# Splitting ScalarE's top-k search into two chains that take turns

## The chip, the cores and the metric

The kernel runs on one core of a Trainium2 chip. The metric is the device time of one execution in microseconds (us), of which the median of several executions is given. A core has TensorE (PE in the profile, its weight loads PEld), VectorE (DVE), ScalarE (ACT), GpSimd (POOL) and SyncE (SP), which here issues the DMA transfers. Each engine works through its own queue in order; a queue whose first instruction waits holds everything behind it.

## The reference

Two transformer layers over 1024 tokens. Layer 0 mixes tokens by two attentions side by side. One of them (the part that matters here) lets each query see only the 256 keys with the highest indexer score:

```python
act = relu(einsum('bqhd,bsd->bqhs', qi, k_idx))
score = einsum('bqhs,bqh->bqs', act, wi)          # one row of up to 1024 scores per query
score = where(chunk_id(s) <= chunk_id(t), score, -inf)
_, sel = lax.top_k(score, 256)
...
o_b = diff_attention(...)                          # softmax(q0 k0) - lambda * softmax(q1 k1): two maps per head
y = concatenate([o_a, o_b]) @ w_out
```

Then, in both layers, follow an output projection, cross attention to a memory and an MLP.

## The kernel before

Queries are worked on in 8 blocks of 128 rows, one row per partition. The first two blocks have at most 256 admissible keys and need no search; the other six have score rows of 384, 512, 640, 768, 896 and 1024 numbers, which lie side by side in the tile `score`. `topk_steps` finds the 256th largest number of each row by a search over the 32 bits of its pattern, from the highest bit down. One bit takes a count over each row (how many scores reach the trial value) and then three tiny operations on VectorE which form the next trial value. `chain` is a generator of such a search over a list of blocks.

There are two chains. The d chain has the three short blocks; VectorE counts them itself (`dve_count`, L482). The a chain has the three long blocks; ScalarE counts them with a Sign activation and an accumulator (`act_count`, L486), and VectorE does the three updates (`tk_ok` L503, `tk_u` L510, `tk_try` L511). ScalarE's first count of a bit needs the `tk_try` of the bit before, and `tk_ok` needs all three counts. When the 32 bits are through, VectorE fixes the threshold (L526 to L534) and `select` makes the mask of each block (L550 to L555 on VectorE, L556 on GpSimd).

The search runs beside the projections of `even_rest`, which need no scores. TensorE does them in halves of 24 matmuls into four PSUM banks (`ps_S`); each half is split into a high part by ScalarE (`z_hi`, L135 or L129) and a low part by VectorE (`z_lo`, L136 or L130) and stored to DRAM by SyncE (L234, L235). The order of projections is qb (4), kb (4), with the small `ka` and `va` groups between, then eight tiles `vb` (L642), then qa (4). Their weights come in by DMA (L117), are rounded by ScalarE (`w_hi`, L120) and split by GpSimd (`w_lo`, L125). Between projections `pump` advances the chains by so many steps each.

Then come the attentions. `diff_units` come first: the scores of a unit are made for two maps one after the other (`scores`, L315, for `s0` and `s1`), reduced on VectorE (L332), exponentiated on ScalarE (L334), joined on GpSimd (L720, L725, L726) and turned by TensorE (L258). `load_qk` brings q and k of one map from DRAM in six transfers (L655 to L659).

What stands in an engine's queue is put in order, when the program is built, by a scheduler that estimates when each instruction could start. So a change in one place also changes the order around it. SBUF tiles of the attentions lie where tiles of the projections were, so a load may have to wait until TensorE is through with those.

Of the kernel before, what the change touches and what calls it, by code (L numbers as in the profile page):

```python
# [12 lines left out]
F32 = mybir.dt.float32  # L13
# [9 lines left out]
P = 128  # L23
# [7 lines left out]
TOPK = 256  # L31
# [37 lines left out]
class Net:  # L69
# [398 lines left out]
    def topk_steps(self, score, mask, offs, pool):  # L468
# [3 lines left out]
        nc = self.nc  # L472
        c = self.const
        nb = NT - BLK0
        ND = 3
        thr = c.tile([P, nb], F32, name="tk_thr")
        view = lambda j: score[:, offs[j + BLK0]:offs[j + BLK0] + P * (j + BLK0 + 1)]
        width = lambda j: P * (j + BLK0 + 1)

        def dve_count(j, t, op, acc):  # L480
            junk = pool.tile([P, 1024], BF16, name="tk_junk", bufs=1)
            nc.vector.tensor_scalar(junk[:, 0:width(j)], view(j), t, None, op0=op, op1=ALU.add, accum_out=acc)  # L482
# [5 lines left out]
        def chain(js, tag, count, limit):  # L488
            n = len(js)
            tr = [c.tile([P, n], I32, name="tk_try%d%s" % (i, tag)) for i in range(2)]  # L490
            ok = c.tile([P, n], I32, name="tk_ok" + tag)
            u = c.tile([P, n], I32, name="tk_u" + tag)
            cnt = c.tile([P, n], F32, name="tk_cnt" + tag)
            cur = tr[0]
            nc.vector.memset(cur, 0)
            for b in range(31, -1, -1):
                for k, j in enumerate(js):
                    count(j, cur[:, k:k + 1].bitcast(F32), cnt[:, k:k + 1])
                yield
                if limit is None:  # L500
                    nc.vector.tensor_scalar(ok, cnt, TOPK - 0.5, None, op0=ALU.is_ge)
                else:
                    nc.vector.tensor_tensor(ok, cnt, limit, ALU.is_le)  # L503
                if b == 31:
                    nc.vector.tensor_scalar(u, ok, 1.0, None, op0=ALU.subtract)
                    nxt = tr[1]
                    nc.vector.tensor_scalar(nxt, u, 1 << 30, None, op0=ALU.bitwise_xor)
                else:
                    nxt = tr[b % 2]
                    nc.vector.scalar_tensor_tensor(u, ok, b, cur, ALU.logical_shift_left, ALU.bitwise_xor)  # L510
                    nc.vector.tensor_scalar(nxt, u, 3 << (b - 1) if b > 0 else 1, None, op0=ALU.bitwise_xor)  # L511
                cur = nxt
                yield
            t = cur.bitcast(F32)
            if limit is None:
                nc.vector.tensor_copy(thr[:, js[0]:js[0] + n], t)
                yield
                for j in js:
                    select(j)
                    yield  # L520
                return

            gt = c.tile([P, n], F32, name="tk_gt" + tag)
            mn = c.tile([P, n], F32, name="tk_mn" + tag)
            for k, j in enumerate(js):
                dve_count(j, t[:, k:k + 1], ALU.is_gt, gt[:, k:k + 1])  # L526
                w = pool.tile([P, 1024], F32, name="tk_w", bufs=1)
                nc.vector.tensor_scalar(w[:, 0:width(j)], view(j), t[:, k:k + 1], 3e38, op0=ALU.is_le, op1=ALU.mult)
                nc.vector.tensor_tensor_reduce(w[:, 0:width(j)], w[:, 0:width(j)], view(j), 1.0, 3.3e38, ALU.add, ALU.min,
                                               accum_out=mn[:, k:k + 1])  # L530
                yield
            nc.vector.tensor_scalar(ok, gt, TOPK - 0.5, None, op0=ALU.is_ge)
            nc.vector.tensor_copy(thr[:, js[0]:js[0] + n], t)
            nc.vector.copy_predicated(thr[:, js[0]:js[0] + n], ok, mn)  # L534
            yield
            for j in js:
                select(j)
                yield
# [17 lines left out]
            nc.gpsimd.tensor_scalar(mask[:, offs[j + BLK0]:offs[j + BLK0] + n], gt[:, 0:n], -1.0, -NEG, op0=ALU.add,  # L556
                                    op1=ALU.mult)

        js_a = list(range(ND, nb))
        lim = c.tile([P, len(js_a)], F32, name="tk_lim")  # L560
        for k, j in enumerate(js_a):
            nc.vector.memset(lim[:, k:k + 1], float(width(j) - 2 * TOPK))
        return (chain(js_a, "a", act_count, lim),
                chain(list(range(ND)), "d", lambda j, t, acc: dve_count(j, t, ALU.is_ge, acc), None))

    def even_rest(self, act, zc, zp, z, topk):
        nc, A = self.nc, self.A

        def pump(*steps):

            for k in range(max(steps)):
                for chain, n in zip(topk, steps):
                    if k < n:
                        next(chain, None)

        def proj(name, k, sc, steps=(5, 6)):
            W = self.load_w(A["ev_fm"][k])
            z.setdefault(name, []).append(self.spill(lambda half: self.proj_half(W, act, half), sc, zp))
            pump(*steps)


        W = self.load_w(A["ev_fm"][5])
        uk = self.load_w(A["ev_uk_uv"], None, zc, 1)
        gkv = zc.tile([P, P], F32, name="gkv")
        nc.sync.dma_start(gkv, A["ev_a_kv_norm"][0:1, :].broadcast_to([P, P]))
        cT = zc.tile([P, S], F32, name="cT")
        for half in range(2):
            nc.scalar.activation(cT[:, half * 512:half * 512 + 512], self.proj_half(W, act, half), AF.Copy)
        ch = zc.tile([P, S], F32R, name="c_hi")
        cl = zc.tile([P, S], F32R, name="c_lo")  # L590
        for c in range(2):
            proj("qb", 6 + c, 0.125)
            pn = self.transpose4(cT[:, 512 * c:512 * c + 512], 4)
            q = self.small(4, name="cq")
            for j in range(4):
                junk = self.smallp.tile([P, 1024], BF16, name="junk", bufs=1)
                nc.scalar.activation(junk[:, 0:P], pn[:, j * P:(j + 1) * P], AF.Square, accum_out=q[:, j:j + 1])
            r = self.rstd(q, 4, 1.0 / P)
            cn = zc.tile([P, 512], F32, name="cn", bufs=1)
            for j in range(4):  # L600
                sl = slice(j * P, (j + 1) * P)
                nc.vector.scalar_tensor_tensor(cn[:, sl], pn[:, sl], r[:, j:j + 1], gkv, ALU.mult, ALU.mult)
            pt = self.transpose4(cn, 4)
            self.split(ch[:, 512 * c:512 * c + 512], cl[:, 512 * c:512 * c + 512], pt)
        z["ka"] = []
        z["va"] = self.dr([NT, P, 1024])

        def ka(p):
            def half_ps(half):
                ps = self.ps("S")  # L610
                sl = slice(half * 512, half * 512 + 512)
                self.mm3(ps, (uk[0][:, p * P:(p + 1) * P], uk[1][:, p * P:(p + 1) * P]), (ch[:, sl], cl[:, sl]), True, True)
                return ps

            z["ka"].append(self.spill(half_ps, 1.0, zp))

        def va(t):
            ps = self.ps("S")
            sl = slice(t * P, (t + 1) * P)
            self.mm3(ps, (ch[:, sl], cl[:, sl]), (uk[0][:, 512:1024], uk[1][:, 512:1024]), True, True)  # L620
            v = zc.tile([P, 8, P], F32R, name="va_st", bufs=2)
            self.split(v[:, :, 0:64], v[:, :, 64:128], ps.rearrange("p (h d) -> p h d", h=8))
            nc.sync.dma_start(z["va"][t], v.rearrange("p h d -> p (h d)").bitcast(F32))

        for k, (name, f, sc) in enumerate([("qb", 8, 0.125), ("qb", 9, 0.125)] + [("kb", 10 + j, 1.0) for j in range(4)]):
            proj(name, f, sc)
            if k < 4:
                ka(k)
                va(2 * k)
                va(2 * k + 1)  # L630
        Wv = [self.load_w(A["ev_vb"][j]) for j in range(4)]
        Wv = [[w.rearrange("p (k f) -> p k f", k=2) for w in pair] for pair in Wv]
        z["vb"] = self.dr([NT, P, 512])
        for t in range(NT):
            ps = self.ps("S")
            a = act[t // 4]
            sl = slice((t % 4) * P, (t % 4) * P + P)
            for kd in range(KD):
                w = Wv[kd // 2]
                self.mm3(ps, (a[0][:, kd, sl], a[1][:, kd, sl]), (w[0][:, kd % 2], w[1][:, kd % 2]), kd == 0, kd == KD - 1)  # L640
            v = zp.tile([P, 512], F32, name="vb", bufs=2)
            nc.scalar.activation(v, ps, AF.Copy)  # L642
            nc.sync.dma_start(z["vb"][t], v)
            pump(3, 4)
        for j in range(4):
            proj("qa", 14 + j, 0.125, (4, 2))
        pump(100, 100)

    def load_qk(self, zq, zk, j, pool):
        nc = self.nc  # L650
# [900 lines left out]
```

## Time and profile before

| | |
|---|---|
| time of the kernel before, median of 3 runs | 2593.91 us (2591.81 to 2595.8) |
| the profiled execution: its own time | 2590.76 us |
| its span, first to last instruction | 2589.0 us |
| busy: TensorE / VectorE / ScalarE / GpSimd | 2415.5 / 1687.6 / 1429.9 / 532.5 us |
| mean granted clock of TensorE | 0.97 of full speed |

Busy time is what an engine spent in its instructions. TensorE is busy for 93% of the span, so the question for any change is where TensorE stands idle, and what it waits for there. The times in the trace count from the start of the span; in each row the number in brackets is the idle time just ahead, with what ended it.

### The profile page before, as it was taken

How to read it: one execution, taken by the hardware profiler on the slowest of the kernel's cores; microseconds unless marked ns; L12 is line 12 of the kernel's file. 1: busy time of each engine (PE TensorE's matmuls, PEld its weight loads, DVE VectorE, ACT ScalarE, POOL GpSimd, SP SyncE). 2: the span in 40 equal slices, each digit the busy share in tenths (PEclk: the TensorE clock that was granted, in tenths of full speed). 3: DMA queues.
4: the chain of work that ended last, by engine and by line, in shares of the span. 5: the costliest groups of instructions: out<-in, count | busy, mean ns of one | idle time of the engine just before them, and what ended most of it. 6: DMA issues, size and time to landing. Idle time of an engine off the chain costs nothing. (4 is left out here: it accounts for less than half of the span.)

```text
span 2589.0 us, 34350 instructions
## 1 busy us (share of the span) xinstructions
PE 2415.5 (93%) x11493; PEld 1972.1 (76%) x11493; DVE 1687.6 (65%) x3184; ACT 1429.9 (55%) x2808; POOL 532.5 (21%) x898
## 2 busy tenths in 40 slices
PE   7999988899997799997999999989979999899998
PEld 6877867688876687875888878878757777688886
DVE  5599676698448755553655768874596555446556
ACT  5577747787356555552434458873565555434433
POOL 5322125545233000000000245541320000000003
PEclk9999989999998899998999999999989999999999
DMA  5225365663423344465776531123233443667665
GB/s 179 82 87 217 129 193 131 149 161 99 159 82 130 103 154 140 146 243 191 248 252 211 195 126 38 38 88 128 82 119 126 148 157 135 226 241 257 226 228 178
DMA packets 165662, 402.78 MB, mean 156 GB/s; under 512 B 20282, under 2 KB 38638, under 8 KB 165486
## 3 DMA queue, kind: packets, MB, share of 16 engines
q1 hardware_dynamic: 165486, 400.59, 46.9%
q8 instruction: 91, 1.49, 0.2%
q14 instruction: 85, 0.70, 0.1%
HBM read 283.47 MB, written 117.05 MB: 155 GB/s over the span
## 5 line engine op out<-in xcount | busy, mean ns | idle before, releaser
L200 POOL TENSOR_SCALAR rstd<-ssq 128x1 f32<-128x1 f32 x48 | 40.5, 844 | 1329.2 <-ACT junk L154 1328.3
L129 ACT ACTIVATE l_hi<-l_raw 128x1024 fp32r<-128x1024 f32 x112 | 118.5, 1060 | 344.2 <-PE ps_T L1259 147.4
L130 DVE TENSOR_TENSOR l_lo<-l_raw,l_hi 128x1024 fp32r<-128x1024 f32 x112 | 136.8, 1223 | 126.0 <-ACT l_hi L129 126.0
L1259 PE MATMUL ps_S<-w_hi,l_hi 128*128 128x512 f32 x480 | 191.4, 399 | 27.2 <-ACT l_hi L129 27.2
L125 POOL TENSOR_TENSOR w_lo<-w_raw,w_hi 128x512 fp32r<-128x512 f32 x118 | 159.5, 1374 | 237.5 <-ACT w_hi L120 221.6
L140 PE MATMUL ps_S<-act_hi,w_hi 128*128 128x512 f32 x512 | 201.6, 395 | 2.5 <-DVE z_lo L130 1.2
L141 PE MATMUL ps_S<-act_lo,w_hi 128*128 128x512 f32 x512 | 200.5, 392 | 1.5 <-DVE act_lo L130 1.5
L142 PE MATMUL ps_S<-act_hi,w_lo 128*128 128x512 f32 x512 | 199.4, 390 | 0.1
L1259 PE MATMUL ps_S<-w_hi,l_lo 128*128 128x512 f32 x480 | 189.0, 396 | 0.0
L1259 PE MATMUL ps_S<-w_lo,l_hi 128*128 128x512 f32 x480 | 188.7, 393 | 0.0
L129 ACT ACTIVATE s_hi<-w_raw 128x512 fp32r<-128x512 f32 x160 | 100.6, 631 | 100.3 <-PE ps_S L1100 83.6
L130 DVE TENSOR_TENSOR s_lo<-w_raw,s_hi 128x512 fp32r<-128x512 f32 x160 | 109.8, 688 | 58.6 <-ACT s_hi L129 45.6
L1259 PEld LDWEIGHTS ps_S<-w_hi,l_hi 128*128 128x128 f32 x480 | 91.6, 191 | 46.9 <-ACT l_hi L129 28.0
L140 PE MATMUL ps_S<-w_hi,act_hi 128*128 128x512 f32 x320 | 124.7, 398 | 2.4 <-DVE yn L198 1.5
L141 PE MATMUL ps_S<-w_lo,act_hi 128*128 128x512 f32 x320 | 126.2, 395 | 0.1
L142 PE MATMUL ps_S<-w_hi,act_lo 128*128 128x512 f32 x320 | 125.6, 393 | 0.0
L140 PEld LDWEIGHTS ps_S<-act_hi,w_hi 128*128 128x128 f32 x512 | 96.2, 188 | 24.4 <-DVE onm L1421 2.3
L141 PEld LDWEIGHTS ps_S<-act_lo,w_hi 128*128 128x128 f32 x512 | 96.3, 188 | 20.6 <-DVE act_lo L130 2.2
L142 PEld LDWEIGHTS ps_S<-act_hi,w_lo 128*128 128x128 f32 x512 | 96.2, 188 | 19.8 <-POOL w_lo L125 0.5
L334 ACT ACTIVATE s<-s,nm 128x128 f32<-128x128 f32 (+7 forms) x128 | 99.1, 778 | 19.3 <-DVE nm L332 18.9
L1259 PEld LDWEIGHTS ps_S<-w_hi,l_lo 128*128 128x128 f32 x480 | 91.2, 190 | 21.5
L1259 PEld LDWEIGHTS ps_S<-w_lo,l_hi 128*128 128x128 f32 x480 | 91.3, 190 | 20.4
(367 smaller groups left out, 7194.1 us busy)
## 6 DMA issues: line engine op xcount, KB each, us to landing
l_raw<-dr SPq DMA_DIRECT2D x112, 512.0 KB, 4.5
dr<-ua SPq DMA_DIRECT2D x192, 256.0 KB, 2.4
w_raw<-w SPq DMA_DIRECT2D x64, 512.0 KB, 3.6
w_lo<-w SPq DMA_DIRECT2D x128, 256.0 KB, 4.1
w_hi<-w SPq DMA_DIRECT2D x128, 256.0 KB, 4.6
x_dram<-xt SPq DMA_DIRECT2D x40, 512.0 KB, 2.9
xt<-x_dram SPq DMA_DIRECT2D x40, 512.0 KB, 3.7
w_raw<-ev_fm SPq DMA_DIRECT2D x18, 512.0 KB, 4.0
```

Source lines behind the costliest of these rows:

```text
L125: nc.gpsimd.tensor_tensor(lo[:, cs], raw[:, cs], hi[:, cs].bitcast(F32), ALU.subtract)
L129: self.nc.scalar.activation(hi, src, AF.Copy)
L130: self.nc.vector.tensor_tensor(lo, src, hi.bitcast(F32), ALU.subtract)
L140: nc.tensor.matmul(ps, lhsT=a[0], rhs=b[0], start=first, stop=False)
L141: nc.tensor.matmul(ps, lhsT=a[0], rhs=b[1], start=False, stop=False)
L142: nc.tensor.matmul(ps, lhsT=a[1], rhs=b[0], start=False, stop=last)
L200: nc.gpsimd.tensor_scalar(r, q[:, 0:1], q[:, 1:2] if n == 2 else 0.0, EPS, op0=ALU.add, op1=ALU.add)
L334: nc.scalar.activation(s[:, 0:n], s[:, 0:n], AF.Exp, bias=nm, scale=-1.0, accum_out=sm)
L1259: nc.tensor.matmul(banks[z][t], lhsT=x[i], rhs=w[j][:, e], start=start and b == 0 and e == 0 and n == 0, stop=b == NB - 1 and e == 1 and n ...
```

## The change

The a chain is cut in two. The new a chain has only the longest block (1024 numbers), the new b chain has the blocks of 768 and 896. `pump` advances a, b and d one step each in turn. The counts stay as they were; the three update operations are now done once for a and once for b in every bit.

```diff
-        js_a = list(range(ND, nb))
-        lim = c.tile([P, len(js_a)], F32, name="tk_lim")
-        for k, j in enumerate(js_a):
-            nc.vector.memset(lim[:, k:k + 1], float(width(j) - 2 * TOPK))
-        return (chain(js_a, "a", act_count, lim),
+        def signs(js, tag):
+            lim = c.tile([P, len(js)], F32, name="tk_lim" + tag)
+            for k, j in enumerate(js):
+                nc.vector.memset(lim[:, k:k + 1], float(width(j) - 2 * TOPK))
+            return chain(js, tag, act_count, lim)
+
+        return (signs([nb - 1], "a"), signs(list(range(ND, nb - 1)), "b"),
                 chain(list(range(ND)), "d", lambda j, t, acc: dve_count(j, t, ALU.is_ge, acc), None))
...
-        def proj(name, k, sc, steps=(5, 6)):
+        def proj(name, k, sc, steps=(5, 5, 6)):
...
-            pump(3, 4)
+            pump(3, 3, 4)
         for j in range(4):
-            proj("qa", 14 + j, 0.125, (4, 2))
-        pump(100, 100)
+            proj("qa", 14 + j, 0.125, (4, 4, 2))
+        pump(100, 100, 100)
```

The order of the queues shows three places. From line 566 on, the lines of the changed kernel stand two higher (L642 is L644 there).

ScalarE's queue in the middle of the search, before: one bit of the a chain is three counts in a row, and the next bit's counts (with the other trial tile) follow at once.

```order
L486 ACTIVATE tk_junk_a,tk_cnta<-score,tk_try0a 128x768
L486 ACTIVATE tk_junk_a,tk_cnta<-score,tk_try0a 128x896
L486 ACTIVATE tk_junk_a,tk_cnta<-score,tk_try0a 128x1024
L642 ACTIVATE vb<-ps_S 128x512
L486 ACTIVATE tk_junk_a,tk_cnta<-score,tk_try1a 128x768
```

The same place of ScalarE's queue now:

```order
L486 ACTIVATE tk_junk_a,tk_cnta<-score,tk_try1a 128x1024
L486 ACTIVATE tk_junk_a,tk_cntb<-score,tk_try1b 128x768
L486 ACTIVATE tk_junk_a,tk_cntb<-score,tk_try1b 128x896
L486 ACTIVATE tk_junk_a,tk_cnta<-score,tk_try0a 128x1024
L486 ACTIVATE tk_junk_a,tk_cntb<-score,tk_try0b 128x768
L486 ACTIVATE tk_junk_a,tk_cntb<-score,tk_try0b 128x896
L644 ACTIVATE vb<-ps_S 128x512
```

Between two counts of a there now stand the two of b, and the other way round. The end of the search has moved too: before, 11 of the 32 bits of a were still to come when the d chain was through, now it is 5 of a and 6 of b; the last count now stands ahead of three of the eight `vb` and of all four `w_hi` of the qa projections.

ScalarE's queue at the end of the search now:

```order
L486 ACTIVATE tk_junk_a,tk_cnta<-score,tk_try1a 128x1024
L486 ACTIVATE tk_junk_a,tk_cntb<-score,tk_try1b 128x768
L644 ACTIVATE vb<-ps_S 128x512
L486 ACTIVATE tk_junk_a,tk_cntb<-score,tk_try1b 128x896
L644 ACTIVATE vb<-ps_S 128x512 x2
L120 ACTIVATE w_hi<-w_raw 128x1024 x2
```

Before, the last six bits stood between and behind these `w_hi`, and the last count stood among the `z_hi` of qa. On VectorE the last operation of `select` stood behind the last `z_lo`, among the first reductions of the scores; now it stands ahead of the last six `z_lo`.

SyncE's queue at the loads of the second map of the first head, before (dr_1879 and dr_1880 are its q, dr_2499 and dr_2500 its k, dr_3599 the second qa projection, dr_3696 the third):

```order
L658 DMA att_kh<-dr_2499 64x1024
L655 DMA att_q<-dr_1879 64x1024
L234 DMA dr_3599<-z_hi 128x1024
L656 DMA att_q<-dr_1880 64x1024
L659 DMA att_kh<-dr_2499 64x1024
L235 DMA dr_3600<-z_lo 128x1024
L658 DMA att_kl<-dr_2500 64x1024
L659 DMA att_kl<-dr_2500 64x1024
L234 DMA dr_3696<-z_hi 128x1024
```

The same loads now (dr_1880 and dr_1881 are q, dr_2536 k, dr_3871 and dr_3872 the fourth and last qa projection):

```order
L660 DMA att_kh<-dr_2536 64x1024
L657 DMA att_q<-dr_1880 64x1024
L234 DMA dr_3871<-z_hi 128x1024
L235 DMA dr_3872<-z_lo 128x1024
L658 DMA att_q<-dr_1881 64x1024
L661 DMA att_kh<-dr_2536 64x1024
```

The second halves of q and k of that map have moved behind the store of the last qa projection's `z_lo`. TensorE's second pair of score matmuls waits for both of them.

## Rows read from the trace of the kernel before

**Rows 1.** Busy time of each engine in two stretches (start:end, length, then us).

```profile
core 0: us, PE busy (x) PEld busy (x) DVE busy (x) ACT busy (x) POOL busy (x), PEclk, DMA share, GB/s
160.00:346.00 186.00, 180.34 (x796) 147.19 (x795) 141.75 (x460) 145.15 (x272) 38.77 (x41) 1.00 0.45 158
160.00:289.00 129.00, 123.39 (x546) 100.36 (x545) 118.77 (x396) 101.05 (x192) 26.33 (x29) 1.00 0.48 178
```

**Rows 2.** Timeline of TensorE, end of projections (start, length, instruction, [idle before]).

```profile
364.94 0.39 PE L142 MATMUL ps_S<-act_hi,w_lo 128*128 128x512 f32 x1
365.17 0.28 PE L315 MATMUL ps_S<-att_kh,att_q 128*128 128x256 f32 x1
...
366.99 0.39 PE L315 MATMUL ps_S<-att_kh,att_q 128*128 128x256 f32 x1 [1.18 <-DVE tk_need L551]
...
374.57 0.58 PE L315 MATMUL ps_S<-att_kh,att_q 128*128 128x256 f32 x1 [7.08 <-DVE tk_need L551]
...
379.45 0.48 PE L258 MATMUL ps_T<-ident,s 128*128 128x128 f32 x1
```

**Rows 3.** Timeline of VectorE at the same place.

```profile
373.83 0.69 DVE L136 SCALAR_TENSOR_TENSOR z_lo<-ps_S,z_hi 128x512 fp32r<-128x512 f32 x1
...
374.49 0.28 DVE L332 CUSTOM_DVE_ANT_0 s<-ps_S,H 128x128 f32<-128x128 f32 x1
...
375.25 1.28 DVE L554 SCALAR_TENSOR_TENSOR tk_eq<-tk_w,tk_need,tk_eq 128x1024 bf16<-128x1024 f32 x1
```

**Rows 4.** Waits from 155 to 375 us (total us, times, longest).

```profile
DVE tk_oka L503 <- ACT tk_junk_a L486: 32.0, 18, 5.2
ACT tk_junk_a L486 <- DVE tk_try1a L511: 17.2, 14, 3.9
ACT tk_junk_a L486 <- DVE tk_try0a L511: 14.0, 10, 3.1
```

**Rows 5.** Timeline of ScalarE: a weight, a vb tile, first counts of two bits.

```profile
319.95 1.04 ACT L120 ACTIVATE w_hi<-w_raw 128x1024 fp32r<-128x1024 f32 x1
...
324.01 0.58 ACT L642 ACTIVATE vb<-ps_S 128x512 f32<-128x512 f32 x1
...
338.08 0.94 ACT L486 ACTIVATE tk_junk_a<-score,tk_try0a 128x768 bf16<-128x768 f32 x1 [0.21 <-DVE tk_try0a L511]
...
342.24 0.94 ACT L486 ACTIVATE tk_junk_a<-score,tk_try1a 128x768 bf16<-128x768 f32 x1 [0.69 <-DVE tk_try1a L511]
```

**Rows 6.** Timeline of VectorE: tiny operations of the chains among counts.

```profile
266.07 0.17 DVE L501 TENSOR_SCALAR tk_okd<-tk_cntd 128x3 int32<-128x3 f32 x1
...
266.68 0.61 DVE L482 TENSOR_SCALAR_CACHE_REDUCE tk_junk<-score,tk_try0d 128x384 bf16<-128x384 f32 x1
...
267.33 0.75 DVE L482 TENSOR_SCALAR_CACHE_REDUCE tk_junk<-score,tk_try0d 128x512 bf16<-128x512 f32 x1
...
268.00 0.16 DVE L503 TENSOR_TENSOR tk_oka<-tk_cnta,tk_lim 128x3 int32<-128x3 f32 x1
268.12 0.88 DVE L482 TENSOR_SCALAR_CACHE_REDUCE tk_junk<-score,tk_try0d 128x640 bf16<-128x640 f32 x1
...
270.99 1.21 DVE L510 SCALAR_TENSOR_TENSOR tk_ud<-tk_okd,tk_try0d 128x3 int32<-128x3 int32 x1
```

**Rows 7.** Timeline of GpSimd: weights of qa, then the first units.

```profile
321.08 5.05 POOL L125 TENSOR_TENSOR w_lo<-w_raw,w_hi 128x512 fp32r<-128x512 f32 x4 [18.57 <-ACT w_hi L120]
...
379.48 1.04 POOL L556 TENSOR_SCALAR mask<-tk_gt 128x1024 bf16<-128x1024 bf16 x1
...
382.38 0.72 POOL L726 TENSOR_TENSOR s<-s 128x256 f32<-128x256 f32 x1
```

**Rows 8.** SyncE's queue: timeline of two issues.

```profile
354.75 0.59 SPq L659 DMA_DIRECT2D att_kl<-dr  x1
...
374.54 0.33 SPq L235 DMA_DIRECT2D dr<-z_lo  x1
```

**Rows 9.** The tile att_q from 325 to 400 us: issue to landing.

```profile
DMA to landing us min/median/max: 4.7/5.1/7.7
```

## The prediction

> **What bounds the kernel now.** I read the page first: TensorE is busy for 93% of the span, so only its idle places can pay. The stretches around the search come next [rows 1]. From 160 to 346 us, while the search runs, TensorE is busy for 180.34 of 186 us: the search costs it almost nothing there. The 5.6 us that it lacks lie all before 289 us, in the `ka` and `va` groups. So a faster search is worth nothing by itself; what counts is what its end holds up. TensorE's timeline shows that [rows 2]: the last projection's matmul starts at 364.94, two pairs of scores follow, one more at 366.99, and then TensorE stands for 7.08 us until 374.57. VectorE's timeline gives the cause [rows 3]: the last `z_lo`, which frees a PSUM bank, starts at 373.83, and the first reduction of scores at 374.49. Up to there VectorE was busy with fixing thresholds and `select` for the three long blocks, which could only start when the a chain was through (about 346.5). The reductions wait in the same queue.
>
> The a chain is late because it runs at neither engine's pace. The list of waits [rows 4] has both sides: VectorE waited 32.0 us for counts, ScalarE 17.2 + 14.0 = 31.2 us for trial values, in 24 waits (1.3 us each).
>
> **The change, part by part.** *ScalarE's waits.* One bit of counts takes 342.24 − 338.08 − 0.69 = 3.47 us without the wait [rows 5], some 1.06, 1.17 and 1.24 us for the three widths. While VectorE updates a, ScalarE now counts b's two blocks (2.2 us), more than the mean wait; while it updates b, it counts a's one (1.24 us), about as much. So most of the 31.2 us goes. It is bounded by 31.2 (all of it) and 0; the long waits (up to 3.9) are only partly covered, and I leave 11 us, a third.
>
> *The end of the chain.* ScalarE was busy for 145.15 us from 160 to 346 [rows 1]. Of that, four `w_hi` (1.04 each), three `vb` and three `z_hi` (about 0.58 each) [rows 5], together 7.7, now stand behind the last count. Idle were 186 − 145.15 = 40.85; 31.2 of it by the chain, 9.65 by other things. So the last count ends at 160 + 137.5 + 9.65 + 11 = 318, bounded by 307 and 338 with none and all of the waits kept.
>
> *VectorE's 96 more tiny operations* (three a bit, 32 bits). Three of them in a row, each waiting for the last, take 266.68 − 266.07 = 0.61, so 0.20 each; one put between two counts costs nothing (a 512 count of 0.75 to the next count: 0.79 with `tk_oka` between; a 384 count of 0.61 to the next: 0.65 without) [rows 6]. That bounds the 96 by 0 and 19.5 us. Most stand between or beside others; I take 0.08 each, 7.7 us. Then the d chain ends at 289 + 8 = 297, and the 5.5 bits left, 5.5 × 3.47 and two `vb`, end at 317. The two ways agree; I take 318, between 307 and 338.
>
> *A row that speaks against it:* `tk_ud` at 270.99 took 1.21 instead of 0.16 us [rows 6], as long as one of GpSimd's four subtractions at 321.08 (5.05 / 4 = 1.26) [rows 7]. GpSimd was busy for 26.33 us of the d chain's 129 [rows 1], the most that such holding can take there. If the added operations were held for half of that, the chain would end 13 us later, at 331. The Trainium skill ("SBUF — State Buffer", section "Who interferes with whom") says that VectorE and GpSimd share a port pair as an exclusive lock, and that the second to start is blocked until the first is done; the 1.21 us agree with it. It makes a rival, below.
>
> *What the new place of the last count holds up.* Behind it stand two `vb`, then the first `w_hi` of qa, then GpSimd's subtraction of its first half: 318 + 2 × 0.58 + 1.04 + 1.26 = 321.5. TensorE needs them when qa begins: 8 halves of 24 matmuls at 180.34 / 796 = 0.2266 us [rows 1] are 43.5, so at 365.2 − 43.5 = 321.7, the low part half a us later. So there is no stall up to 318.8 for the last count; each us beyond costs one.
>
> *The end of the search.* From the last count to the end of `select` VectorE took some 32 us before (346.5 to 378.6, evictions included), so it now ends by about 350. The last `z_lo` follows its `z_hi` at once. TensorE's last matmul ends at 365.3, `z_hi` 0.6 later, so `z_lo` runs from 366.0 to 366.7 instead of 373.83 to 374.52: 7.8 us earlier.
>
> *What is late next.* The first unit needs the second map, and two of that map's loads now stand in SyncE's queue behind the store of that last `z_lo`. Before, the last load of that map was issued at 354.75 and the store, at 374.54, right when `z_lo` ended, held up nothing of it [rows 8]. Now: store at 366.7, `att_q` at 367.1, `att_kh` at 367.6, and 5.1 us to landing (4.7 to 7.7) [rows 9], so the second pair of scores starts at about 372.6 (371.8 to 374.8). Everything behind it on TensorE waits too. The removed wait of 7 us has a successor of almost the same length.
>
> *What is left.* Before, two more pairs had been made by then, so TensorE came from the fourth pair at 374.57 to the first turn of a unit at 379.45 [rows 2]. From 372.6 it has two pairs of some 0.5 us more and one at the end (0.45) less to do, so it comes there at about 378.0: 1.4 us earlier. The second unit gains more: `select`'s 1.28 us [rows 3] no longer stands among the reductions, and the mask of 1.04 us at 379.48 no longer stands ahead of GpSimd's joins [rows 7]. Its join, ended at 383.1 before, should end at about 378.5: 4.6 us. GpSimd paces the next units, and I take 3.5 us, between 1.4 and 4.6, as what lasts.
>
> *The sum:* 2590.76 − 3.5 + 0 (stall) = 2587.3 for the profiled execution, whose time is 3.15 below the median of the runs; against that median, 2593.91 − 3.5 = **2590.4 us**, 0.13% less. A difference under 0.2% (5.2 us) is about what a measurement here cannot tell from none.
>
> **The rivals.**
> - *The full gain.* Nothing takes the place of the wait: the loads come sooner than I think, or SyncE's queue is not held. Then the first reductions move with `z_lo`, and 374.49 − 365.6 = 8.9 us is gained: 2585.0. For it: VectorE's wait really goes. Against: the order of SyncE's queue. If the 5.6 us of the `ka` and `va` groups went too, 2579; but VectorE, whose `z_lo` they wait for, has more to do there, not less. Chance 0.25.
> - *The chain ends late (slower).* The tiny operations are held behind counts and behind GpSimd's subtractions, so ScalarE's waits stay. From 318.8 each us of delay stalls TensorE at the first qa weights. From 322.3 the gain is eaten, from 327.5 the kernel is slower by over 0.2%; at 331 (13 us of holding) it is 2593.9 − 3.5 + 12.2 = 2602.6. For it: the held `tk_ud` and the in-order queue. Against: VectorE was busy for 118.77 of 129 us [rows 1] with room for half of what is added, and the b chain's counts give each update 2.2 us. Chance 0.15. The lock that the Trainium skill states ("SBUF — State Buffer", "Who interferes with whom") would be what holds them.
> - *No gain at all.* The loads take the 7.7 us that one of them took, the second pair starts at 374.8, and the ramp is as before: 2593.9. The search is faster for nothing. Chance 0.15.
> - *My forecast:* 0.45.
>
> **How the numbers follow.** The likeliest case gives 2590.4, its own range 2588 to 2594. Eight in ten take in the full gain (2585, and a little below for the spread of the medians) and the first part of the late chain: 2583 to 2598. Faster by over 0.2%: the full gain and a bit of the forecast's edge, 0.28. Slower: the late chain, 0.15, less what of it ends before 327.5 and more for changes of order further on, 0.15. The rest, 0.57, is no change.
>
> **What the profile after would show.** Right: ScalarE's waits for trial values fall from 31 to about 11 us; the last count ends near 318; VectorE is through with `select` by 350; the last `z_lo` starts near 366; TensorE still stands for about 7 us after the first pair of scores, now for a load of `att_q` or `att_kh`. Wrong: a stall of TensorE at the first qa weights (late chain), or pairs of scores that follow the first without a gap (full gain), or more idle time in the `ka` and `va` groups than 5.6 us.

## The result, and the profile after

The changed kernel takes 2608.64 us (median of 4 runs, 2606.68 to 2609.68), the kernel before 2593.35 (4 runs, 2591.81 to 2595.8). The ratio is 1.0057, with a 95% interval of 1.004 to 1.0075: slower by 0.57%, some 15 us. The prediction was 2590.4, no change, in a range from 2583 to 2598. It was wrong.

The profiled execution took 2609.68 us, 18.9 more than the one of before (the medians are 15.3 apart, so some 3.6 of it belong to these two executions). Cut at the same places of the program in both traces (the first and last starts of a group of matmuls), the difference falls like this:

| stretch of TensorE | before | after | difference |
|---|---|---|---|
| start to the last indexer score | 158.8 | 160.1 | +1.3 |
| search beside projections, to the first attention score | 206.4 | 212.4 | +6.0 |
| attentions, to the last score | 257.5 | 257.6 | +0.1 |
| even output projection, to the first cross-attention score | 119.4 | 124.7 | +5.3 |
| the rest | 1846.9 | 1853.1 | +6.2 |

The last row holds several us that vary between executions: with the same order of instructions it was 1846.9 before, and 1851.9 (e7) and 1849.1 (e9) in two experiments below. The search and the output projection are the two that stand out, and the attentions, where something was to be gained.

First the search. In the waits of the kernel after from 155 to 375 us (total, times, longest) the chains do what the change says:

```profile
DVE tk_okb L503 <- ACT tk_junk_a L486: 6.3, 10, 2.0
...
ACT tk_junk_a L486 <- DVE tk_oka L503: 4.4, 6, 1.1
ACT tk_junk_a L486 <- DVE tk_ua L510: 3.7, 2, 2.5
...
DVE tk_oka L503 <- ACT tk_junk_a L486: 2.9, 6, 0.7
```

VectorE waits 9.2 us for counts instead of 32.0, ScalarE 10.8 us for the chain instead of 31.2 [rows 4] (the 8.1 of these lines and four more waits of 0.4 to 1.0). The busy times after, in the second stretch of [rows 1] and in two short ones (the column of 0.97 is the granted clock of TensorE; an x counts every instruction that overlaps the stretch):

```profile
160.00:289.00 129.00, 120.42 (x516) 96.96 (x515) 121.58 (x477) 114.39 (x218) 26.18 (x30) 0.97 0.45 166
210.90:214.30 3.40, 3.40 (x10) 2.63 (x9) 3.40 (x12) 3.21 (x8) 0.00 (x0) 0.51 0.62 213
262.10:265.50 3.40, 3.40 (x9) 2.63 (x10) 3.40 (x13) 1.00 (x2) 0.00 (x0) 0.51 0.85 201
```

Up to 289 us ScalarE is busy for 114.39 us, 13 more than before: the counts that used to come later come now. In the same 129 us TensorE made 516 matmuls instead of 546. ScalarE's timeline shows how the two hang together:

```profile
207.39 0.58 ACT L135 ACTIVATE z_hi<-ps_S 128x512 fp32r<-128x512 f32 x1
207.87 1.03 ACT L486 ACTIVATE tk_junk_a<-score,tk_try0b 128x896 bf16<-128x896 f32 x1
...
208.90 0.58 ACT L129 ACTIVATE z_hi<-ps_S 128x512 fp32r<-128x512 f32 x1
209.37 0.59 ACT L129 ACTIVATE c_hi<-ps_T 128x512 fp32r<-128x512 f32 x1
...
315.00 1.03 ACT L486 ACTIVATE tk_junk_a<-score,tk_try1b 128x896 bf16<-128x896 f32 x1
...
372.68 0.60 ACT L135 ACTIVATE z_hi<-ps_S 128x512 fp32r<-128x512 f32 x1 [4.84 <-PE ps_S L142]
...
663.81 1.06 ACT L120 ACTIVATE w_hi<-w_raw 128x1024 fp32r<-128x1024 f32 x1 [8.72 <-DMA w_raw<-ev_out]
```

A count of the b chain, whose trial value is there already, stands at 207.87 between two evictions. The `c_hi` at 209.37, which TensorE needs, ends one count later than it could. TensorE's timeline after, at this and later places:

```profile
210.02 0.50 PE L140 MATMUL ps_S<-c_hi,w_hi 128*128 128x512 f32 x1 [2.82 <-ACT c_hi L129]
...
228.23 0.50 PE L140 MATMUL ps_S<-w_hi,c_hi 128*128 128x512 f32 x1 [1.29 <-DVE z_lo L136]
...
261.96 0.66 PE L140 MATMUL ps_S<-act_hi,w_hi 128*128 128x512 f32 x1 [1.34 <-DVE z_lo L130]
...
265.71 0.40 PE L140 MATMUL ps_S<-act_hi,w_hi 128*128 128x512 f32 x1
...
372.48 0.28 PE L315 MATMUL ps_S<-att_kh,att_q 128*128 128x256 f32 x1
...
382.86 0.55 PE L315 MATMUL ps_S<-att_kh,att_q 128*128 128x256 f32 x1 [9.98 <-DMA att_kh<-dr]
...
664.91 0.80 PE L140 MATMUL ps_S<-w_hi,act_hi 128*128 128x512 f32 x1 [3.46 <-ACT w_hi L120]
...
1762.47 0.80 PE L140 MATMUL ps_S<-w_hi,act_hi 128*128 128x512 f32 x1 [5.35 <-DVE yn L198]
```

Six waits in the `ka` and `va` groups (2.82, 1.29, 0.88, 1.06, 0.93 and 1.34 us) make 8.3; before, five made 5.5 (1.25, 1.05, 1.05, 1.95 and 0.17). Behind the first and the last of the six the granted clock is 0.51 for 3.4 us, the lower of its two levels (1.2 of 2.4 GHz). The matmuls start 0.43 us apart there: nine steps from one start to the next take 3.75 us from 261.96 to 265.71, and nine take 3.65 from 210.82 to 214.47. At 0.2266 us a step the 18 would take 4.1 us, so 3.3 more are lost. 2.8 + 3.3 make up the 6.0. Before, the clock stayed at 1.00 in both places.

The counts are not the whole of it. Ahead of the last two of these waits VectorE's own queue is late:

```profile
257.69 2.53 POOL L125 TENSOR_TENSOR w_lo<-w_raw,w_hi 128x512 fp32r<-128x512 f32 x2 [12.86 <-ACT w_hi L120]
```

```profile
257.94 1.06 DVE L510 SCALAR_TENSOR_TENSOR tk_ua<-tk_oka,tk_try1a 128x1 int32<-128x1 int32 x1
258.92 0.68 DVE L130 TENSOR_TENSOR z_lo<-ps_S,z_hi 128x512 fp32r<-128x512 f32 x1
```

The `z_hi` of this half is through at 258.10. But `tk_ua`, which takes 1.06 us where most take 0.16, ends only when the first of GpSimd's two subtractions does (257.69 + 1.26), and `z_lo` starts at 258.92; TensorE's wait of 0.93 us at 259.65 is for it. Ahead of the last wait it is a held `tk_okd` (0.72 us) and a count of 0.61 us that stand before the `z_lo`. From 200 to 270 us five such operations took 3.5 us more than usual after the change, two took 1.7 before.

VectorE's timeline after has the other end of the search:

```profile
208.90 1.18 DVE L510 SCALAR_TENSOR_TENSOR tk_ud<-tk_okd,tk_try1d 128x3 int32<-128x3 int32 x1
...
349.02 0.62 DVE L555 TENSOR_TENSOR tk_gt<-tk_gt,tk_eq 128x896 bf16<-128x896 bf16 x1
...
373.31 0.69 DVE L136 SCALAR_TENSOR_TENSOR z_lo<-ps_S,z_hi 128x512 fp32r<-128x512 f32 x1
...
1761.72 1.29 DVE L198 TENSOR_TENSOR yn<-ps_S,g 128x512 f32<-128x512 f32 x2 [4.98 <-DMA g<-norm_g]
```

`select` is through at 349.6, and the last `z_lo` follows its `z_hi` (372.68) at once. Nothing of the search holds up the first scores any more, [rows 3] are gone. But at the handover from the projections to the scores the wait of 7.08 us in [rows 2] has become one of 9.98 us, up to 382.86, for `att_kh`. SyncE's queue after, at this place and ahead of the output projection (an entry with x6 is six issues of one line in a row):

```profile
372.45 0.45 SPq L660 DMA_DIRECT2D att_kh<-dr  x1
372.99 0.55 SPq L657 DMA_DIRECT2D att_q<-dr  x1
373.63 0.54 SPq L234 DMA_DIRECT2D dr<-z_hi  x1
374.21 0.42 SPq L235 DMA_DIRECT2D dr<-z_lo  x1
374.69 0.45 SPq L658 DMA_DIRECT2D att_q<-dr  x1
375.19 1.32 SPq L661 DMA_DIRECT2D att_kh<-dr  x1
...
629.87 0.33 SPq L159 DMA_DIRECT2D g<-norm_g  x1
630.79 18.89 SPq L117 DMA_DIRECT2D w_raw<-ev_out  x6
...
651.37 8.13 SPq L934 DMA_DIRECT2D xk<-dr  x8
659.61 0.52 SPq L117 DMA_DIRECT2D w_raw<-ev_out  x1
```

Even the two loads of the second map that stand *ahead* of the stores are issued only at 372.45, when the last projection's matmuls end; the two stores then take 1.1 us of the queue (373.63 to 374.69), and the last load 7.7 us from its issue to the scores. So it is the end of the projection that holds this queue, not the `z_lo` store alone.

And the weights of the output projection come late: before, three of the eight were loaded ahead of the norm weights (at 518.67, 593.80 and 614.63), now one (at 599.36). Six follow the load of `g`, which waits for TensorE for 11.0 us, and the last one stands behind nine `xk` loads (one earlier, and these eight). That is the 8.72 us wait of `w_hi` at 663.81 and TensorE's 3.46. In layer 1 it is the load of `g` itself that comes later: it stands behind ten `xk` loads and one weight, before behind eight `xk` loads. It is issued 1.3 us ahead of TensorE's wait (at 1755.83, the wait begins at 1757.12), before 3.5 us (1742.56 and 1746.08), and `yn` gets it 5.9 us after its issue, before 4.2. So `yn` waits for it until 1761.72, and TensorE 5.35 us instead of 1.46.

### The profile page after: what moved, and what is told of

Its sections match the earlier page's. It is cut to its first block, busy times and chain, and to the rows that moved or that the text cites. A ratio compares the mean times of both kernels' runs of the same rounds, so it can differ in the third digit from the quotient of the medians.

```text
span 2607.9 us, 34466 instructions
## 1 busy us (share of the span) xinstructions
PE 2421.0 (93%) x11478; PEld 1979.2 (76%) x11493; DVE 1695.0 (65%) x3284; ACT 1430.5 (55%) x2808; POOL 536.7 (21%) x898
## 5 line engine op out<-in xcount | busy, mean ns | idle before, releaser
L141 PE MATMUL ps_S<-act_lo,w_hi 128*128 128x512 f32 x512 | 202.1, 395 | 2.0 <-DVE act_lo L130 2.0
```

What stands on the lines that cost most here:

```text
L141: nc.tensor.matmul(ps, lhsT=a[0], rhs=b[1], start=False, stop=False)
```

## The experiments

Two things beside the chains differ in the changed program. **The order:** the scheduler laid all queues anew, behind the search too. **The addresses:** the chains' small constant tiles take 256 bytes more per partition (eight slots of 32). What is laid out behind them moves up by 256, while the weight buffers, counted from the other end of the SBUF, stay. In the built programs:

```
                          before              after
att_q,  map 0             122848              123104
att_q,  map 1             126944              127200
att_kh, map 1             143328              143584
w_lo of the last qa       131040 (both; 4096 bytes long)
w_hi of the last qa       147424 (both)
```

Before, 122848 was exactly the start of a weight buffer, and 126944 + 4096 = 131040 ends where the next one starts. After, the buffers of map 1 reach 256 bytes into those of the last qa projection, so their loads must wait until it is through. Three theories, then, each of which can hold for one part: the chains themselves (ScalarE and VectorE too full for evictions), the order, the addresses.

In the experiments "before's order" means that, outside the search, each engine's queue is pinned to the order of the kernel before by dependencies that only order instructions of one engine:

```diff
         Net(tc, A, out).run()
+        pin(tc, nc)      # for each engine, over the wanted order:
+                         #   tc.add_manual_dep(i, prev.name, info, reason="order")
```

**Two chains, before's order** (`e1_two_old_order`), all but eight instructions of the first two output weights, which stay free.

> Two chains as in the changed kernel, but every instruction outside the search stands on its engine in the order of the kernel before (all but the 8 of the first two weight loads of the even output projection, which are left to the scheduler). Theory 'order': the two chains shorten the search as worked out, and the 15 us were lost because the scheduler laid the rest of the program out in another order (about 6 us of it from 160 to 372 us, 5 in the even output projection, 4 to 6 in the odd one). Then this comes to 2586-2596 us. Rival 'chains': the second chain itself is the loss, by its 96 added updates on VectorE and by counts that keep ScalarE from the evictions. Then it stays at 2602 us or more.

2623.15 us, ratio 1.0111 (1.0094 to 1.0129). Slower than the change itself, and as neither theory had it. Of its waits from 320 to 395 us, one of SyncE's and one of TensorE's:

```profile
SPq L657 <- PE ps_S L142: 27.1, 1, 27.1
...
PE ps_S L315 <- DMA att_kh<-dr: 17.0, 1, 17.0
```

A load of `att_q`, placed where it could go before, now waits 27.1 us for TensorE's projection, and all of the queue behind it waits too. This is what led to the addresses. (The free instructions cost something of their own further on, about 9 us at 654.)

**One chain, after's order** (`e2_one_new_order`): the program of before, with its addresses, in the order of after.

> One chain on ScalarE as in the kernel before, but every instruction outside the search in the order of the changed kernel. Theory 'order': 2602-2610 us, with the waits of the two output projections (3.5 us for w_hi, 5 us for yn) in the trace. Rival 'chains': 2591-2597 us.

2607.04 us, ratio 1.0055 (1.004 to 1.0071), nearly that of the change, without it. TensorE's waits in it:

```profile
PE ps_S L315 <- DMA att_kh<-dr: 23.4, 4, 12.3
PE ps_S L140 <- DVE yn L198: 6.7, 3, 4.9
PE ps_S L140 <- ACT w_hi L120: 6.5, 4, 4.2
```

The handover, `w_hi` and `yn`: all three late waits of after, from its order alone. Of the 12.3 us at the handover about half is still the late end of the one chain: the store of `z_lo` goes at 374.94, and the scores follow 5.8 us later, behind the loads. The search stretch takes 208.1 us, 1.7 more than before.

**The change, before's order late only** (`e3_two_old_order_late`, from the third output weight on) **and early only** (`e4_two_old_order_search`, ahead of the attentions).

> The changed kernel, with the order of the kernel before from the third weight load of the even output projection to the end; search and attention are left as in the changed kernel. Theory 'order': what was lost in the two output projections comes back, 8 to 11 us, so 2598-2601 us. Rival 'chains': same time as the changed kernel within 3 us.

> The changed kernel, with the order of the kernel before for all that stands ahead of the attention (outside the search); attention and all that follows are left as in the changed kernel. Theory 'order': the 6 us between 160 and 372 us come back, so about 2602 us, and TensorE has no waits over 2 us there. Rival 'chains': the evictions stand behind ScalarE's counts in this order too, and the 6 us stay.

2604.93 us, 1.0046 (1.0033 to 1.0059), and 2608.46, 1.0059 (1.0046 to 1.0072): the first less of a gain than the theory of the order had asked for, the second none. The late order takes the `yn` wait from 5.35 to 1.77 us; the handover (9.9 us) and the output projection (124.6) stay. The early order brings nothing: the stretch of the search takes 213.4 us and its waits remain (2.8 for `c_hi`, 5.7 + 1.7 for `z_lo`). So the order that the change brought is not what makes them.

**Addresses alone.** A filler tile ahead of the buffers makes up for the 256 bytes (64 × 4), or adds them to the kernel before:

```diff
-                    self.pool(s1, "gap").tile([P, 528], F32, name="gap")
+                    self.pool(s1, "gap").tile([P, 464], F32, name="gap")   # e5, e7, e9; 592 in e6
```

`e5_two_gap464` is the change with 464, `e6_one_gap592` the kernel before with 592, both laid out by the scheduler; `e7_two_gap464_old_order` is e5 in before's order.

> The changed kernel with the filler ahead of the attention's buffers 64 numbers shorter (464 for 528), so that the buffers of q and k lie again on the addresses that they had before: each exactly on one weight buffer, not across two. Theory 'address': the change made the constants 256 bytes longer, which pushed each attention buffer across two weight buffers, so that its load must wait for the later of both, and part of the 15 us is this. Then the wait for att_kh after the projections falls from 10 us to 5 us or less and the time to 2596-2604 us. Rival 'order': the scheduler's new order is the whole loss; then 2605 us or more, with the wait as long as before.

> The kernel before (one chain), with the filler 64 numbers longer (592 for 528): the attention's buffers lie where the changed kernel has them, across two weight buffers each. Theory 'address': slower than before by 4 to 12 us, with a wait for att_q or att_kh of 8 us or more at the start of the attention. Rival 'chains' (the second chain alone is the loss): 2591-2597 us.

> Two chains, the filler of 464, and every instruction outside the search in the order of the kernel before: of the change only the two chains are left. If address and order are the whole loss: 2586-2594 us (up to 8 us gained at the start of the attention). If the two chains delay the evictions between 200 and 262 us as in the changed kernel (6 us): 2592-2600 us, with those waits in the trace and without those of the output projections.

| | time | ratio (95%) | search | attentions | output projection | rest |
|---|---|---|---|---|---|---|
| e5 | 2614.13 | 1.0075 (1.0063 to 1.0087) | 212.4 | 243.6 | 119.6 | 1877.5 |
| e6 | 2630.42 | 1.014 (1.0122 to 1.0158) | 206.2 | 252.3 | 125.8 | 1881.3 |
| e7 | 2593.92 | 0.9996 (0.9984 to 1.0008) | 214.0 | 246.8 | 119.6 | 1851.9 |

With the addresses back (e5) the wait at the handover is gone and the attentions take 14 us less, and the scheduler itself lays the output weights well again: 119.6. With the kernel before moved by 256 bytes (e6) the handover waits 8.0 us for `att_kh`, and the last output weight stands behind nine `xk` loads, as in after: 125.8. (The wait costs e6 nothing there: its one chain holds up the last `z_lo` until 374.73, and the scores go on at 374.53. Its attentions even take 5.2 us less than before.) So both come from the addresses, the second by way of the order that the scheduler makes of them. e1 and e7 have the same chains and, but for the eight instructions, the same order: 29 us apart, 17 of them up to the first score (231.1 against 214.0) and 11 in the output projection, where the eight are. Both e5 and e6 lose far more in the MLPs, where their new orders put a wait that neither before nor after has (18.4 us in e5, 23.5 in e6; e5's waits of TensorE):

```profile
PE ps_S L1102 <- ACT w_hi L129: 18.4, 13, 1.9
```

e7 puts a price on the chains by themselves: none. What the handover gives, the search and the varying rest take: in before's own order and addresses the attentions take 10.7 us less than before, the stretch of the search 7.6 more and the rest 5.0 more. Its TensorE waits from 200 to 270 us:

```profile
PE ps_S L140 <- DVE z_lo L130: 4.7, 3, 2.3
PE ps_S L140 <- DVE z_lo L136: 3.2, 1, 3.2
PE ps_S L140 <- ACT c_hi L129: 2.8, 1, 2.8
```

**The order of SyncE's queue, pinned in two places** (`e8_two_pins`: the change, with the loads of `g` behind the second output weight and `xk` behind the last).

```diff
+            early = self.w_dma                # load of the second output weight
...
+            self.last_w = self.w_dma
+            with self.tc.issue_after(early.ins):
+                g1, g2 = ...
...
+            with self.tc.issue_after(self.g_dma.ins), self.tc.issue_after(self.last_w.ins):
                 nc.sync.dma_start(k[...], zk...)
```

> The changed kernel with a few loads held in the order that they had before on SP: in both output projections the loads of the norm's weights behind the second weight load, and the loads of xk behind the last weight load and the norm's weights. Theory 'order' for the output projections: the waits for w_hi at 655 to 665 us (4 us) and for yn at 1762 us (5 us) go, so 2598-2602 us. Rival: the weights come late for another cause (the slots that they wait for); then 2605 us or more.

2656.77 us, 1.023 (1.0209 to 1.0251). Inconclusive for its question: the pins made the scheduler lay out the MLPs in yet another way, with 26 of the waits that e5 has 13 of (36.2 us). The `w_hi` wait falls to 2.4, the `yn` wait stays at 4.6.

**Addresses back, before's order from the first cross attention on** (`e9_two_gap464_old_order_late`): e5 without its bad MLPs.

> Two chains, the filler of 464, search and even attention in the order that the scheduler gives them; from the first cross-attention on every instruction in the order of the kernel before. Where the order alone lost the time after 733 us (in the run with the filler of 464 the first cross-attention began at 734 us, 8 us earlier than in the kernel before, and the MLP then waited 13 times for w_hi), this keeps the 8 us: 2583-2590 us. If those waits come from the earlier start or the addresses and not from the order: 2605 us or more.

2586.66 us, 0.9973 (0.9961 to 0.9984): the two chains as they could have been. SyncE's queue in e9, and TensorE's timeline (start, length, instruction):

```profile
350.33 0.65 SPq L660 DMA_DIRECT2D att_kh<-dr  x1
351.08 0.54 SPq L657 DMA_DIRECT2D att_q<-dr  x1
...
352.78 1.06 SPq L658 DMA_DIRECT2D att_q<-dr  x1
353.89 1.40 SPq L661 DMA_DIRECT2D att_kh<-dr  x1
```

```profile
372.12 0.28 PE L315 MATMUL ps_S<-att_kh,att_q 128*128 128x256 f32 x1
...
372.35 0.28 PE L315 MATMUL ps_S<-att_kh,att_q 128*128 128x256 f32 x1
```

The loads of map 1 go out 20 us before the scores need them, and the scores follow without a gap.

**The search held back** (`e10_two_throttled`): e9, but in the `ka` and `va` groups the chains' steps stand on ScalarE and VectorE behind the last evictions of the step.

```diff
-            proj(name, f, sc)
+            proj(name, f, sc, (0, 0, 0) if k < 4 else (5, 5, 6))
...
+                a, d = self.last_split           # the two evictions of the step's last va
+                with self.tc.issue_after(a.ins), self.tc.issue_after(d.ins):
+                    pump(5, 5, 6)
```

> The run before, and in the four projections between which ka and va are made, the counts and updates of a step are queued behind the evictions of that step's last va on ScalarE and VectorE. Theory 'two chains keep ScalarE full, and the evictions of ka and va stand behind a count': TensorE's waits of 1 to 3 us from 205 to 265 us (8 us in all) fall to 5 us or less, as with one chain, and the time is 3 to 6 us under that of the run before. Rival: they come from VectorE's added updates or from POOL and stay; same time within 2 us.

2584.49 us, 0.9965 (0.9953 to 0.9977). Its waits of TensorE from 200 to 270 us, its busy times up to 289 us, and TensorE's first scores:

```profile
PE ps_S L140 <- DVE z_lo L136: 0.6, 1, 0.6
PE ps_S L140 <- DVE z_lo L130: 0.6, 1, 0.6
```

```profile
160.00:289.00 129.00, 127.59 (x566) 104.28 (x566) 102.37 (x399) 102.23 (x193) 26.36 (x29) 1.00 0.49 180
```

```profile
364.29 0.38 PE L315 MATMUL ps_S<-att_kh,att_q 128*128 128x256 f32 x1 [2.52 <-DVE z_lo L136]
...
369.51 0.58 PE L315 MATMUL ps_S<-att_kh,att_q 128*128 128x256 f32 x1 [4.72 <-DVE nm L332]
```

566 matmuls in the 129 us, 20 more than before and 50 more than after, at full clock. The search stretch falls from 213.3 us in e9 to 202.1. The waits fell as the theory asked (5 us or less), the time by only 2.2 us instead of 3 to 6, which is within the spread of both kernels' runs. For the search ends later (last count at 336.5 instead of 315.0), and the first pairs of scores wait again, 7.2 us: the old bottleneck is back, and most of the gain goes there (the attentions take 251.9 instead of 243.6).

**Held back on one engine only** (`e11_throttled_act` with `a.ins`, `e12_throttled_dve` with `d.ins`).

> As the run with the queued counts, but only ScalarE's counts are queued behind the last va eviction of their step; VectorE's counts and updates run freely. Theory 'the evictions stand behind ScalarE's counts': TensorE's waits from 205 to 265 us stay gone (2 us in all or less) and the search ends earlier than at 336 us, since VectorE isn't held; 2578-2585 us. Rival 'VectorE's added updates and counts hold z_lo': 4 us or more of waits come back, 2585-2588 us.

> The same with only VectorE's counts and updates queued behind the last va eviction of their step, ScalarE's counts run freely. Theory 'ScalarE's counts': waits of 5 us or more are back, 2584-2588 us. Rival 'VectorE': the waits stay under 3 us.

2585.02 us, 0.9964 (0.995 to 0.9978), and 2586.41, 0.9971 (0.9961 to 0.9981): both like e10. By the conditions set ahead neither came out for ScalarE's counts alone: e11's waits (3.8 us) lie between the two theories, and e12's (2.7) meet the one for VectorE. But a chain goes back and forth between the two engines, so holding it on one slows it on the other, and in e12 both are relieved (ScalarE busy for 99.93, VectorE for 101.31 us up to 289). e11 says more: ScalarE is down to 100.97 us and VectorE as full as in after (121.61; 120.59 in e9), and the waits fall from 9.6 us in e9 to 3.8. That speaks for ScalarE's load as the larger part. It does not show it, since VectorE's updates follow the counts and so came at other times too: held operations took 2.6 us more than usual from 200 to 270 us in e11, 3.5 in e9, 0.6 in e10 and e12. What VectorE's load alone would make was not isolated.

## Why the prediction was wrong

Right, by its own steps:

- *ScalarE's waits*, "I leave 11 us": 10.8.
- *The end of the chain*, last count "ends at 318": it starts at 315.00 and takes 1.03, so it ends at 316.0. The d chain's threshold is formed at 293.01, by the forecast at 297: 3.6 us later than before, so the 96 added operations cost VectorE less than the 7.7 us taken.
- *What the new place of the last count holds up*, "no stall": TensorE has none between 262 and 372.
- *The end of the search*, "by about 350": 349.6.
- The rival of the late chain fell: the search ended 2 us ahead of the forecast. Operations are held, as the `tk_ud` of 1.18 us at 208.90, which agrees with the port lock of the Trainium skill ("SBUF — State Buffer", "Who interferes with whom"). But of the 282 tiny operations after, 13 took over 0.3 us (7.3 us more than usual together), of the 188 before, 11 (8.1 us): no more over the whole search. What neither the rival nor the forecast saw is where they fall: in the `ka` and `va` groups they rose from two to five, ahead of evictions, and there they delay not the chain but TensorE.

Right in the mechanism, wrong in its cause and size:

- *The end of the search*, last `z_lo` "from 366.0": it runs right behind its `z_hi`, but at 373.3, since TensorE came 7.3 us later.
- *What is late next*: TensorE stands behind the first pair for a load of `att_kh`, as said, but for 9.98 us instead of about 7. The step took two loads behind the `z_lo` store, at once after it and 5.1 us to landing. The last one did go 2.5 us after the last matmul's end (372.65 to 375.19; forecast 365.3 to 367.6), but it needed 7.7 us to the scores instead of 5.1, which is most of the difference. And all four loads, not two, wait for the last qa projection, whose weight buffers theirs now overlap by 256 bytes. Either cause brings a wait by itself: the order with before's addresses (e2, 5.8 of its 12.3 us) or the addresses with before's order (e1, 17.0). With both mended (e5, e9) it is gone, and more than the 8.9 us of the rival *the full gain* comes at this place: the attentions take 14 us less, and e9, though its search stretch is 6.9 us longer, is at 2586.7. I held the rival down to 0.25 by the order of SyncE's queue, without asking why the scheduler put the loads so late.
- *What is left*, "3.5 us", "as what lasts": nothing, the attentions take 257.6 us instead of 257.5.

Failed: **the sum**, "2590.76 − 3.5 + 0 (stall)". Its steps end at about 383 us, and it has no term for what lies before 318 or behind.

- Before: "the search costs it almost nothing there" was read off the trace of a search that ScalarE had to wait in. Those 31 us of waits were the slack in which evictions could pass. The change fills them, and evictions stand behind a count of 1 us, on VectorE also behind held updates: +6.0 us, 2.8 in waits and some 3.3 at the lower clock behind them. That it is the chains and not the order or addresses is shown by e4 and e7 (the waits stay) and e10 (they go when counts and updates are held back); how much of it is ScalarE's and how much VectorE's is open. The prediction even named it as a sign to look for ("more idle time in the `ka` and `va` groups"), without a price.
- Behind: +5.3 us in the even output projection, and 3.9 of the last 6.2 in the `yn` wait, both from SyncE's queue laid anew. The prediction had looked at the order at three places and left the rest to a clause, "more for changes of order further on". e2 shows that the order alone makes such a loss, e5 and e6 that the addresses make the order at the output projection.

The parts of the change, then: the chains alone, 0 (e7: 0.9984 to 1.0008); order and addresses as they fell out, +15. Open are the several us by which the stretch from the first cross attention to the end varies, so that only the 3.9 us there are accounted for; and whether a search held back less than in e10, so that it ends before the scores need it, keeps both gains. e10's 2584.5 is the lowest of all here.

## What to carry to other kernels

A wait inside an engine off the critical path may be the slack that lets its urgent work pass: before filling it, price what stands in that queue behind the new work, and keep the filler behind the evictions (e10). Where a scheduler and an allocator lay out the program, a change of a few instructions is also a change of every address behind it and of every queue: compare buffer overlaps and DMA queues over the whole program, and test the edit once with addresses and order restored, or its own worth can't be seen. An experiment that restores only one of the two can be worse than both kernels (e1, e5).

## What the runs showed of the hardware

A pause of TensorE can cost more than its length: behind waits of 2.82 and 1.34 us (0.93 shortly before the second) the granted clock stood at 0.51 for 3.4 us, and the matmuls came 0.43 us apart (3.75 us for the nine steps from 261.96 to 265.71) instead of 0.23. Behind the waits of 1.25 and 1.95 us of before, at the same places of the program, it stayed at 1.00. So it did in e9 behind a wait of 2.81 us, as long as the first of these (1.00 from 209 to 213 us), so the length of one pause does not settle it. The two levels are those of the Trainium skill ("TensorE: Matmul & The Clock Gate", "Part 1: The HAM clock gate").

A tiny operation of VectorE can be held by GpSimd: the `tk_ud` of 208.90 ends at 210.08 and the subtractions of GpSimd that it ran beside at 210.07 (207.57 + 2.50); `tk_ua` of 257.94 ends at 259.00 and the first of the two there at about 258.96.
